# Attention stage of a hybrid decoder step: loads and splits of a group apart, two turned blocks ahead, stores issued by GpSimd, other weights

## The chip, the core and the metric

The kernel runs on one core of a Trainium2 chip. A core has a matrix engine (TensorE, in the profile PE for its matmuls and PEld for its weight loads), three engines for elementwise work (VectorE or DVE, ScalarE or ACT, GpSimd or POOL) and SyncE (SP), which here only issues DMAs. Each engine works through its own queue of instructions strictly in order; an instruction that waits for a semaphore holds up everything behind it on its engine. DMAs can be issued from the queues of SP, ACT and POOL. The metric is the time of one execution on the device in microseconds (us), lower is better.

## What is computed

One inference step of two layers for a prompt of 2048 tokens and, beside it, for 8 decode sequences of 4 new tokens each with 2048 past tokens. Layer 0 has two groups of heads in parallel: HGRN2 (linear attention) and forgetting attention ("fox"); layer 1 is GLA. The change is in the fox attention. Its prompt part and its decode part are:

```python
def fox_prompt(q, k, v, log_f):                    # 4 heads of 128, 2048 tokens
    c = jnp.cumsum(log_f, axis=1).swapaxes(1, 2)
    logits = jnp.einsum('bthd,bshd->bhts', qi, k) * scale + ci[..., None] - c[:, :, None, :]
    logits = jnp.where(t[:, None] >= key_pos[None, :], logits, -jnp.inf)
    p = jax.nn.softmax(logits, axis=-1)
    return jnp.einsum('bhts,bshd->bthd', p, v)

def fox_sample(q, k, v, log_f, k_pages, v_pages, logf_pages, page_table):
    k_past = k_pages[page_table].reshape(db, -1, H, dh)     # 16 pages of 128 rows for each sequence
    v_past = v_pages[page_table].reshape(db, -1, H, dh)
    ...
    p = jax.nn.softmax(jnp.concatenate([logit_past, logit_new], axis=-1), axis=-1)
    return jnp.einsum('bhts,bshd->bthd', p[..., :P], v_past) + jnp.einsum('bhts,bshd->bthd', p[..., P:], v)
```

The outcome is multiplied by a SiLU gate and goes into the output projection of layer 0.

## The kernel before

The program has three phases: the even layer's projections and its HGRN2 heads, then the fox attention (`phase_fox`, L1113), then the output projection of layer 0 and the whole of layer 1. Precision comes from splitting fp32 numbers into two fp16 parts, high and low; a product is then three fp16 matmuls (`mm3`, L450 to L454: high by high, high by low, low by high). Every split is an ACT copy to fp16 and a subtraction of it.

Order. The code writes instructions in program order; a scheduler in the framework then builds the queue of each engine from a simulated timeline, taking among the instructions that are ready the one that stands first in the program. So the order in a queue can differ from the program's. Three tools steer it: `high_priority` puts instructions ahead of all others, `issue_after(x)` keeps what follows behind instruction x in the queue of x's engine (for instructions on that engine alone), and the weights of `mux`, which interleaves two generators: each `yield` gives a cost, and the side whose share of its total (FOX_P for the prompt, FOX_S for the decode part) is behind goes next.

The prompt (`fox_prompt`) runs over 16 groups, 4 heads h by 4 row blocks G of 512 rows. For each group it loads q, k, v (`raw`, 256 KB each, by SP), the bias `cb` and the gate `fsg`, and splits q, k, v (`load_split`, L1131: ACT L1142 and L1143, GpSimd L1144; v is first multiplied on ACT by `self.sv`, a power of two that `y_bounds` works out from the largest |v|, a chain over DVE and PE). `loads` for the next group is called after the first of the group's four blocks of 128 rows. `scores` makes for each block the logits (tile `s`, PE), adds the bias and takes the running maximum on DVE (L1189, with `cm` from GpSimd, L1175), the exponentials on ACT (L1197), and normalises on GpSimd (L1205). `values` turns the probabilities by PE transposes into PSUM (`pt`, L1225, two buffers), splits them (`th` ACT L1232, `tl` DVE L1233) and multiplies them with v (`fo`); it keeps one turned block ahead of the one being multiplied (two, once the decode part has been emitted). The values of a group are interleaved with the scores of the next. The result times the gate (`fy`, DVE L1247) is stored to DRAM (`yT`, L1249) from ACT's queue, the two half-groups at the very end from GpSimd's.

The decode part (`fox_sample`) reads 128 K pages and 128 V pages of 256 KB (SP, L1310; 27 buffers `pg`). Four pages of one sequence make a "quad": 16 PE transposes (`pkt`, L1339), four copies to SBUF (`kts`, ACT L1342 for even heads, DVE L1343 for odd ones), then four sums side by side on the PE array (`sc`, L1397). Once four quads are turned, `past` builds the decay terms; after all 32 quads comes the softmax. Then 34 "strips" (`pv`, L1473) multiply with the V pages, four pages each, as soon as these have landed. `strips` gives the sums `sc` and `pv` high priority.

The mux costs are S0 12000 before the first load, SC_C for each head of a quad, PV_C for each strip; the prompt's costs are about its PE time in ns.

Of the kernel before, what the change touches and what calls it, by code (L numbers as in the profile page):

```python
# [19 lines left out]
P = 128  # L20
# [13 lines left out]
S0 = 12000.0  # L34
SC_C = 700.0
Z_C = 4000.0
# [10 lines left out]
GATE = -9  # L47
PG = 27
PAST = 12
NG = 2  # L50
WSPLIT = 4
FOX_S = 335000.0
FOX_P = 270000.0
# [5 lines left out]
DEC = 4500.0  # L59
PV_C = 4600.0  # L60
NEG = -1e30
# [41 lines left out]
class Kern:  # L103
# [6 lines left out]
    def consts(self):  # L110
        nc, i = self.nc, self.i
        cp = self.ctx.enter_context(self.tc.tile_pool(name="const", bufs=1))
        self.cp = cp

        def col(name, ap, n):
            t = cp.tile([P, n], F32, name=name)
            with nc.allow_non_contiguous_dma(reason="small constant vectors"):
                nc.sync.dma_start(t, ap.rearrange("(k p) -> p k", p=P))
            return t

        self.ident = cp.tile([P, P], F32, name="ident")
# [6 lines left out]
        self.kc, self.n_kc, self.scales = cp.tile([P, 176], F32, name="kc"), 0, {}  # L128
# [108 lines left out]
    def kcol(self, n=1):  # L237
        self.n_kc += n
        assert self.n_kc <= 176
        return self.kc[:, self.n_kc - n : self.n_kc]  # L240
# [209 lines left out]
    def mm3(self, ps, lh, rh, first, last):  # L450
        nc = self.nc
        nc.tensor.matmul(ps, lh[0], rh[0], start=first, stop=False)  # L452
        nc.tensor.matmul(ps, lh[0], rh[1], start=False, stop=False)  # L453
        nc.tensor.matmul(ps, lh[1], rh[0], start=False, stop=last)  # L454

# [318 lines left out]
    def even_half(self, hf, act, wpool, wp, pps, npool, S):  # L774
# [94 lines left out]
        def mk_bkv(hp, which):  # L869
# [74 lines left out]
    def phase_even(self):  # L944
# [4 lines left out]
        with pool("act", side="right") as ap, pool("w", side="right") as w0, pool("wl", side="right") as wp1, \  # L949
# [5 lines left out]
            nrm = Pool(n0, {"th": 1, "nss": 4, "rs_t": 4, "rs_r": 4})  # L955
            self.scales2, self.ready, self.fsc, self.logit = {}, {}, {}, {}
            self.sx_even = self.gain_scale(self.g_even, pps, "pj", "e")
# [155 lines left out]
    def phase_fox(self):  # L1113
        tc, nc = self.tc, self.nc
        with tc.tile_pool(name="fe", bufs=2, reuse_waits="tile") as f1, \
                tc.tile_pool(name="fx", bufs=2, reuse_waits="tile") as f0, \
                tc.tile_pool(name="fpa", bufs=2, space=PSUM, reuse_waits="tile") as pp1, \
                tc.tile_pool(name="fpb", bufs=2, space=PSUM, reuse_waits="tile") as pp0:
            fx = Pool(f0, {"vh": 5, "vl": 5, "P": 17, "th": 3, "tl": 3, "sg": 2, "y": 1},
                      Pool(f1, {"raw": 6, "caus": 1, "qh": 2, "ql": 2, "kh": 5, "kl": 5, "cb": 2, "st1": 12, "cm": 2}))  # L1120
            pps = Pool(pp0, {"t": 2, "o": 1, "kt": 2}, Pool(pp1, {"s": 2, "sc": 1}))
            caus = fx.tile([P, P], F32, tag="caus", name="caus")
            nc.gpsimd.memset(caus, 0.0)
            nc.gpsimd.affine_select(caus, caus, [[-1, P]], ALU.is_ge, FAR, base=0, channel_multiplier=1)
            self.y_bounds(pps)
            with tc.tile_pool(name="fs", bufs=1, side="right", reuse_waits="tile") as s0:
                fs = Pool(s0, {"pg": PG, "kt": 8})
                prompt = self.fox_prompt(fx, pps, caus)
                drain(mux(prompt, FOX_P, self.fox_sample(fs, pps), FOX_S))

    def load_split(self, fx, src, nm, tag, scale=None):  # L1131

        nc = self.nc
        r = fx.tile([P, 512], F32, tag="raw", name=f"raw_{nm}")
        if len(src.shape) == 3:
            nc.sync.dma_start(r.rearrange("p (c d) -> p c d", d=src.shape[2]), src)
        else:
            nc.sync.dma_start(r, src)
        hi = fx.tile([P, 512], F16, tag=tag + "h", name=f"h_{nm}")
        lo = fx.tile([P, 512], F16, tag=tag + "l", name=f"l_{nm}")  # L1140
        if scale is not None:
# [5 lines left out]
    def fox_prompt(self, fx, pps, caus):  # L1147

        nc = self.nc
        cbs, K, V, Q, SG = {}, {}, {}, {}, {}  # L1150
        self.turns = []
        self.sample_done = False

# [7 lines left out]
        def loads(h, G):  # L1161
            gs = slice(G * 512, (G + 1) * 512)
            Q[h, G] = self.load_split(fx, self.qTd[h][:, gs], f"q{h}{G}", "q")
            K[h, G] = self.load_split(fx, self.kTd[h][:, gs], f"k{h}{G}", "k")
            bias(h, G)
            vsrc = self.vd[gs, h * P : (h + 1) * P].rearrange("(c s) d -> s c d", s=P)
            V[h, G] = self.load_split(fx, vsrc, f"v{h}{G}", "v", self.sv[:, 0:1])
            SG[h, G] = fx.tile([P, 512], F32, tag="sg", name=f"fsg{h}{G}")
            nc.sync.dma_start(SG[h, G], self.sgd[h][:, gs])

        def scores(h, G, b):
# [7 lines left out]
            for j in range(G + 1):  # L1179
                w = 512 if j < G else (b + 1) * P  # L1180
                ps = pps.tile([P, 512], F32, tag="s", name=f"s{h}{tb}{j}")
                self.mm3(ps[:, :w], q, [x[:, :w] for x in K[h, j]], True, True)
                lt = fx.tile([P, 512], F32, tag="P", name=f"L{h}{tb}{j}")
# [12 lines left out]
            for j, (lt, w) in enumerate(L):  # L1196
                nc.scalar.activation(lt[:, :w], lt[:, :w], AF.Exp, bias=nm[:, 0:1], scale=ib,  # L1197
                                     accum_out=nm[:, 2 + j : 3 + j])
            if G:
# [8 lines left out]
        def values(h, G, rows, po, b1, b2):  # L1208
# [27 lines left out]
            nj = -(-ns // per)  # L1236
            ahead = [turn(j) for j in range(2 if alone else 1)]
            for j in range(nj):
# [3 lines left out]
                for s, a, c0 in parts:  # L1242
                    vv = [x[:, (s % 4) * P : (s % 4 + 1) * P] for x in V[h, s // 4]]
                    self.mm3(po[:, c0:c2], vv, [x[:, a : a + c2 - c0] for x in (th, tl)], s == 0, s == ns - 1)
                yield sum(c2 - c0 for _, _, c0 in parts) * 2.1
            y = fx.tile([P, 512], F32, tag="y", name=f"fy{h}{G}{b1}")
            nc.vector.scalar_tensor_tensor(y[:, c1:c2], po[:, c1:c2], self.sv[:, 2:3], SG[h, G][:, c1:c2], ALU.mult,  # L1247
                                           ALU.mult)
            (nc.scalar if c2 - c1 == 512 else nc.gpsimd).dma_start(self.yT[0][NH + h][:, G * 512 + c1 : G * 512 + c2], y[:, c1:c2])  # L1249

        groups = [(h, G) for h in range(NH) for G in range(4)]
        loads(0, 0)
        pv, ns = iter(()), 0
# [29 lines left out]
    def fox_sample(self, fs, pps):  # L1283
# [118 lines left out]
        for n in range(4 * DB + 1):  # L1402
            if n < 4 * DB:
# [91 lines left out]
    def fox_scale(self, which, hp):  # L1495


        nc = self.nc
        c = self.scales[f"B{which}{hp}"][:, 2:3]
        up, down = self.fsc[which, hp] = self.kcol(), self.kcol()  # L1500
        nc.vector.tensor_scalar(down, c, 2.0**19, 2.0**-20, ALU.mult, ALU.max)
        if which == "q":
            nc.vector.tensor_scalar(up, c, 2.0**20, 2.0**-19, ALU.mult, ALU.min)
            nc.vector.tensor_scalar(up, up, SCALE, None, ALU.mult)
            return
        nc.vector.reciprocal(up, down)

        ib, beta = self.logit[hp] = self.kcol(), self.kcol()
# [3 lines left out]
    def y_bounds(self, pps):  # L1512
# [17 lines left out]
        most(f, ("Bg0", "Bg1"))  # L1530
        vm, self.sv = self.spread(self.vmax[:, :NPG], pps, "kt", "vm"), self.kcol(3)
        nc.vector.tensor_scalar(f, f, vm, 0.5, ALU.mult, ALU.mult)

        self.power2(vm, 2.0**14, self.sv)
        nc.vector.tensor_scalar(self.sv[:, 2:3], self.sv[:, 1:2], 2.0**-15, None, ALU.mult)
        nc.vector.tensor_tensor(f, f, b, ALU.max)
# [370 lines left out]
```

## Time and profile before

| | us |
|---|---|
| median of 3 runs | 2438.14 (2437.21 to 2438.71) |
| the profiled execution | 2438.64 |
| its span, first to last instruction | 2436.6 |
| mean granted TensorE clock | 0.987 |

The fox stage lies between about 880 and 1332 us of the span. In the rows below, a view by windows gives for each stretch its length and then for each engine the busy time and the number of instructions, then the granted clock, the mean busy share of the DMA engines and GB/s. A view of waits has engine, line and tile that waited, what it waited for, the total in us, how often, and the longest. A timeline row has start, length, engine, line, operation and, in brackets, the idle time of the engine before it and what ended it.

### The profile page before, as it was taken

The numbers are of one execution on the slowest core, as the hardware profiler recorded it, in microseconds if no ns is written. First come the engines' busy times: TensorE is split into PE (matmuls) and PEld (weight loads), VectorE is DVE, ScalarE is ACT, GpSimd is POOL, SyncE is SP. The second block draws the span as 40 slices with busy tenths as digits, with TensorE's granted clock in tenths as the row PEclk, the third lists the DMA queues.
The fourth block names the chain that finished last, engine by engine and source line by source line (L and its number), as shares of the span: only waits on it lengthen the run. The fifth ranks groups of instructions, "written<-read, shape, count | busy, mean of one in ns | idle before, by whom it ended". The sixth has DMA issues, their size and how long they took to land. (4 is left out here: it accounts for less than half of the span.)

```text
span 2436.6 us, 54263 instructions
## 1 busy us (share of the span) xinstructions
PE 2314.2 (95%) x21116; PEld 1642.6 (67%) x21116; DVE 1459.8 (60%) x3337; ACT 1141.4 (47%) x2513; POOL 750.2 (31%) x825
## 2 busy tenths in 40 slices
PE   7999999999999989999788999999999999998998
PEld 5667668855655876666345776777778766666887
DVE  7666656446765637777557353665675555557564
ACT  6434343343433137766457454445553645545243
POOL 2223223012213225443334220432443222322233
PEclk9999999999999999999999999999999999999999
DMA  6222235435431277666684631222146312114454
GB/s 178 78 80 70 76 104 171 144 106 141 148 114 59 85 230 257 207 191 212 224 261 143 198 107 44 62 75 75 63 143 186 125 36 67 47 58 152 141 195 152
DMA packets 297955, 316.96 MB, mean 130 GB/s; under 512 B 39729, under 2 KB 241010, under 8 KB 297698
## 3 DMA queue, kind: packets, MB, share of 16 engines
q1 hardware_dynamic: 295234, 308.98, 40.5%
q8 instruction: 166, 2.72, 0.5%
q10 hardware_dynamic: 2160, 3.93, 0.4%
q14 instruction: 91, 0.75, 0.1%
q0 software_dynamic: 304, 0.59, 0.1%
HBM read 242.31 MB, written 71.11 MB: 129 GB/s over the span
## 5 line engine op out<-in xcount | busy, mean ns | idle before, releaser
L452 PE MATMUL pt_o<-w_o,act 128*128 128x256 f16 x1024 | 282.9, 277 | 2.4 <-ACT w_o L334 1.4
L453 PE MATMUL pt_o<-w_o,act 128*128 128x256 f16 x1024 | 283.2, 277 | 0.9 <-POOL w_o L335 0.9
L454 PE MATMUL pt_o<-w_o,act 128*128 128x256 f16 x1024 | 283.2, 277 | 0.0
L452 PEld LDWEIGHTS <-act 128*128 128x128 f16 (+1 forms) x2320 | 229.0, 99 | 41.7 <-issue 10.7
L453 PEld LDWEIGHTS <-act 128*128 128x128 f16 (+1 forms) x2320 | 228.8, 99 | 33.5 <-issue 2.9
L454 PEld LDWEIGHTS <-act 128*128 128x128 f16 (+1 forms) x2320 | 228.8, 99 | 33.0 <-issue 4.4
L454 PE MATMUL pt_Cv<-w_Cv,act 128*128 128x256 f16 (+1 forms) x520 | 142.4, 275 | 0.0
L452 PE MATMUL pt_Cv<-w_Cv,act 128*128 128x256 f16 (+1 forms) x520 | 142.2, 275 | 0.0
L453 PE MATMUL pt_Cv<-w_Cv,act 128*128 128x256 f16 (+1 forms) x520 | 142.0, 275 | 0.0
L631 POOL TENSOR_TENSOR kA<-kA,fA 128x512 f32<-128x512 f32 (+1 forms) x56 | 80.4, 1436 | 197.3 <-PE gl_A L597 112.5
L631 POOL TENSOR_TENSOR kC<-kC,fC 128x512 f32<-128x512 f32 (+1 forms) x56 | 84.5, 1509 | 157.2 <-PE gl_C L597 76.6
L1197 ACT ACTIVATE L<-L,nm,kc 128x512 f32<-128x512 f32 (+3 forms) x160 | 118.2, 741 | 30.5 <-DVE nm L1195 26.0
L1205 POOL TENSOR_SCALAR L<-L,nm 128x512 f32<-128x512 f32 (+3 forms) x160 | 97.9, 628 | 95.4 <-DVE nm L1201 34.2
L1232 ACT ACTIVATE th<-pt 128x512 f16<-128x512 f32 (+3 forms) x159 | 82.0, 527 | 86.8 <-PE pt L1225 76.7
L1233 DVE TENSOR_TENSOR tl<-pt,th 128x512 f16<-128x512 f32 (+3 forms) x159 | 95.2, 608 | 42.4 <-ACT th L1232 40.9
L1339 PEld LDWEIGHTS pkt<-ident,pgcache_fox_k 128*128 128x128 f32 x512 | 60.1, 144 | 45.6 <-issue 24.8
L1339 PE MATMUL pkt<-ident,pgcache_fox_k 128*128 128x128 f32 x512 | 78.4, 282 | 10.8 <-DMA pgcache_fox_k<-in_cache_fox_k 5.3
L1225 PE MATMUL pt<-ident,L 128*128 128x128 f32 x544 | 88.1, 276 | 0.0
L1225 PEld LDWEIGHTS pt<-ident,L 128*128 128x128 f32 x544 | 68.0, 143 | 22.3 <-issue 1.2
L452 PE MATMUL pt_Bv<-w_Bv,act 128*128 128x256 f16 (+2 forms) x264 | 72.2, 273 | 0.0
L454 PE MATMUL pt_Bv<-w_Bv,act 128*128 128x256 f16 (+2 forms) x264 | 72.2, 273 | 0.0
L453 PE MATMUL pt_Bv<-w_Bv,act 128*128 128x256 f16 (+2 forms) x264 | 72.2, 273 | 0.0
(1088 smaller groups left out, 6863.3 us busy)
## 6 DMA issues: line engine op xcount, KB each, us to landing
pgcache_fox_k<-in_cache_fox_k SPq DMA_DIRECT2D x128, 256.0 KB, 4.1
pgcache_fox_v<-in_cache_fox_v SPq DMA_DIRECT2D x128, 256.0 KB, 3.6
yr<-yT SPq DMA_DIRECT2D x16, 1024.0 KB, 5.8
nx<-in_x_prompt SPq DMA_DIRECT2D x16, 512.0 KB, 5.1
wr_Aqf<-in_w_in_even SPq DMA_DIRECT2D x64, 128.0 KB, 2.8
wr_o<-in_w_out_even SPq DMA_DIRECT2D x32, 256.0 KB, 4.0
wr_Cv<-in_w_in_odd SPq DMA_DIRECT2D x32, 256.0 KB, 4.2
wr_Cqk<-in_w_in_odd SPq DMA_DIRECT2D x64, 128.0 KB, 2.6
```

The lines of the kernel that those rows point to most:

```text
L452: nc.tensor.matmul(ps, lh[0], rh[0], start=first, stop=False)
L453: nc.tensor.matmul(ps, lh[0], rh[1], start=False, stop=False)
L454: nc.tensor.matmul(ps, lh[1], rh[0], start=False, stop=last)
L631: nc.gpsimd.tensor_tensor(kv[:, :, 0], kv[:, :, 0], t1.to_broadcast([P, nb, w]), ALU.mult)
L1197: nc.scalar.activation(lt[:, :w], lt[:, :w], AF.Exp, bias=nm[:, 0:1], scale=ib, accum_out=nm[:, 2 + j : 3 + j])
L1205: nc.gpsimd.tensor_scalar(lt[:, :w], lt[:, :w], nm[:, 1:2], 2.0**14, ALU.mult, ALU.mult)
L1225: nc.tensor.transpose(pt[:, w : w + P], rows[b][s // 4][0][:, (s % 4) * P : (s % 4 + 1) * P], self.ident)
L1232: nc.scalar.activation(th[:, a:w], pt[:, a:w], AF.Copy),
L1233: nc.vector.tensor_tensor(tl[:, a:w], pt[:, a:w], th[:, a:w], ALU.subtract)))
L1339: nc.tensor.transpose(pk[:, j * P : (j + 1) * P], pgs[j][:, h * P : (h + 1) * P], self.ident)
```

## The change

Loads and splits of a prompt group become two functions. The loads stay after the first block of the group before; the splits of q and k are emitted after its third block, that of v after its fourth. Each is placed behind the last exponentials emitted so far (`last_exp`) and behind the last K copy of head 2 emitted so far by the decode part (`last_kt`); both are ACT instructions, so the rule binds ACT's queue. v is scaled by a factor known from the weights (`fox_scale("v", ..)`, worked out in the even phase) instead of one from the measured maximum, and `y_bounds` moves from the start of the stage into the decode part, behind `past`. `values` keeps two turned blocks ahead from the start, with `th` and `tl` in 4 buffers instead of 3. All stores of `fy` are issued by GpSimd. The gate tile `fsg` gets 3 buffers instead of 2, and the pages 25 instead of 27. SC_C goes from 700 to 800, PV_C from 4600 to 5860, FOX_S from 335000 to 411000. `last_pe` is recorded in `scores` and `values`; nothing in the program reads it, and `strips` is as it was.

```diff
-SC_C = 700.0
+SC_C = 800.0
-PG = 27
+PG = 25
-FOX_S = 335000.0
+FOX_S = 411000.0
-PV_C = 4600.0
+PV_C = 5860.0
...
-                if which == "k" and hf == 0:
-                    self.fox_scale("k", hp)
+                if hf == 0:
+                    self.fox_scale(which, hp)
...
-            fx = Pool(f0, {"vh": 5, "vl": 5, "P": 17, "th": 3, "tl": 3, "sg": 2, "y": 1},
+            fx = Pool(f0, {"vh": 5, "vl": 5, "P": 17, "th": 4, "tl": 4, "sg": 3, "y": 1},
...
-            self.y_bounds(pps)
...
-    def load_split(self, fx, src, nm, tag, scale=None):
...
+    def load(self, fx, src, nm):
+        r = fx.tile([P, 512], F32, tag="raw", name=f"raw_{nm}")
+        self.nc.sync.dma_start(r.rearrange("p (c d) -> p c d", d=src.shape[2]) if len(src.shape) == 3 else r, src)
+        return r
+
+    def split(self, fx, r, nm, scale=None):
...
-            Q[h, G] = self.load_split(fx, self.qTd[h][:, gs], f"q{h}{G}", "q")
-            K[h, G] = self.load_split(fx, self.kTd[h][:, gs], f"k{h}{G}", "k")
+            raw["q"] = self.load(fx, self.qTd[h][:, gs], f"q{h}{G}")
+            raw["k"] = self.load(fx, self.kTd[h][:, gs], f"k{h}{G}")
             bias(h, G)
-            vsrc = self.vd[gs, h * P : (h + 1) * P].rearrange("(c s) d -> s c d", s=P)
-            V[h, G] = self.load_split(fx, vsrc, f"v{h}{G}", "v", self.sv[:, 0:1])
+            raw["v"] = self.load(fx, self.vd[gs, h * P : (h + 1) * P].rearrange("(c s) d -> s c d", s=P), f"v{h}{G}")
...
+        def split(which, h, G):
+
+            with ExitStack() as st:
+                for x in (self.last_exp, self.last_kt):
+                    if x is not None:
+                        st.enter_context(self.tc.issue_after(x.ins))
+                r = self.split(fx, raw[which], f"{which}{h}{G}", self.fsc["v", h // 2][0] if which == "v" else None)
+                {"q": Q, "k": K, "v": V}[which][h, G] = r
...
-            ahead = [turn(j) for j in range(2 if alone else 1)]
+            ahead = [turn(j) for j in range(min(2, nj))]
...
-            (nc.scalar if c2 - c1 == 512 else nc.gpsimd).dma_start(self.yT[0][NH + h][:, G * 512 + c1 : G * 512 + c2], y[:, c1:c2])
+            nc.gpsimd.dma_start(self.yT[0][NH + h][:, G * 512 + c1 : G * 512 + c2], y[:, c1:c2])
...
                 rows.append((yield from scores(h, G, b)))
-                if b == 0 and j + 1 < len(groups):
-                    loads(*groups[j + 1])
+                if j + 1 < len(groups):
+                    if b == 0:
+                        loads(*groups[j + 1])
+                    elif b == 2:
+                        split("q", *groups[j + 1])
+                        split("k", *groups[j + 1])
+                    elif b == 3:
+                        split("v", *groups[j + 1])
...
                     new.append(turn(c, b, h, pgs))
+                    if h == 2:
+                        self.last_kt = new[-1][1]
                     yield SC_C
...
             if n == PAST // NH:
                 yield from past()
+                self.y_bounds(pps)
```

More of the change, by code (lines that the diff above doesn't have):

```diff
@@ L126, in consts @@
         self.g_even = col("g_even", i["norm_even"][0], KT)
-        self.kc, self.n_kc, self.scales = cp.tile([P, 176], F32, name="kc"), 0, {}
+        self.kc, self.n_kc, self.scales = cp.tile([P, 184], F32, name="kc"), 0, {}
         self.vmax = cp.tile([P, NPG], F32, name="vmax")
@@ L453, in mm3 @@
         nc.tensor.matmul(ps, lh[0], rh[1], start=False, stop=False)
-        nc.tensor.matmul(ps, lh[1], rh[0], start=False, stop=last)
+        return nc.tensor.matmul(ps, lh[1], rh[0], start=False, stop=last)
     def proj_fm(self, pps, act, W, off, M, hf, evac, nm):
@@ L1129, in phase_fox @@
                 drain(mux(prompt, FOX_P, self.fox_sample(fs, pps), FOX_S))
-    def load_split(self, fx, src, nm, tag, scale=None):
-        nc = self.nc
[L1134 to L1140, printed above, removed]
+    def load(self, fx, src, nm):
[3 more added lines that the diff above has]
+    def split(self, fx, r, nm, scale=None):
+        nc = self.nc
+        hi = fx.tile([P, 512], F16, tag=nm[0] + "h", name=f"h_{nm}")
+        lo = fx.tile([P, 512], F16, tag=nm[0] + "l", name=f"l_{nm}")
         if scale is not None:
@@ L1149, in fox_prompt @@
         nc = self.nc
-        cbs, K, V, Q, SG = {}, {}, {}, {}, {}
+        cbs, K, V, Q, SG, raw = {}, {}, {}, {}, {}, {}
         self.turns = []
-        self.sample_done = False
+        self.sample_done, self.last_exp, self.last_kt = False, None, None
         def bias(h, g):
@@ L1181, in scores @@
                 ps = pps.tile([P, 512], F32, tag="s", name=f"s{h}{tb}{j}")
-                self.mm3(ps[:, :w], q, [x[:, :w] for x in K[h, j]], True, True)
+                self.last_pe = self.mm3(ps[:, :w], q, [x[:, :w] for x in K[h, j]], True, True)
                 lt = fx.tile([P, 512], F32, tag="P", name=f"L{h}{tb}{j}")
@@ L1506, in fox_scale @@
         nc.vector.reciprocal(up, down)
+        if which == "v":
+            self.v_undo[hp] = self.kcol()
+            nc.vector.tensor_scalar(self.v_undo[hp], down, 2.0**-15, None, ALU.mult)
+            return
         ib, beta = self.logit[hp] = self.kcol(), self.kcol()
@@ L1530, in y_bounds @@
         most(f, ("Bg0", "Bg1"))
[L1531 to L1535, printed above, removed]
+        nc.vector.tensor_scalar(f, f, self.spread(self.vmax[:, :NPG], pps, "kt", "vm"), 0.5, ALU.mult, ALU.mult)
         nc.vector.tensor_tensor(f, f, b, ALU.max)
```

15 lines of the change are left out of this document (9 added, 6 removed).

## Prediction

> **What bounds the kernel now.** I read the page first, then busy time by stage, then the waits, then the queues of the engines that the change touches.
>
> ```profile
> span 2436.6 us, 54263 instructions
> PE 2314.2 (95%) x21116; PEld 1642.6 (67%) x21116; DVE 1459.8 (60%) x3337; ACT 1141.4 (47%) x2513; POOL 750.2 (31%) x825
> ...
> 1330.85 0.52 ACT act L1569
> ```
>
> The last row is the first piece of the chain of waits. The chain runs from 1330.9 us to the end, 1105.7 us, and all of it lies behind the fox stage, in code that the change leaves alone. So I take the time after the stage as fixed and ask when the stage ends. By stretches (length, then PE, PEld, DVE, ACT, POOL busy, clock, DMA share, GB/s):
>
> ```profile
> 880.00:905.00 25.00, 15.18 (x123) 12.27 (x121) 10.59 (x55) 9.63 (x19) 11.24 (x13) 0.85 0.98 319
> 905.00:1085.00 180.00, 174.75 (x1249) 113.07 (x1247) 133.90 (x399) 126.66 (x287) 86.62 (x144) 0.98 0.69 223
> 1085.00:1152.00 67.00, 63.65 (x490) 40.83 (x492) 47.74 (x146) 46.16 (x105) 33.17 (x50) 1.00 0.71 225
> 1152.00:1166.00 14.00, 13.28 (x117) 8.28 (x106) 11.31 (x40) 9.46 (x20) 2.92 (x5) 1.00 0.21 74
> 1166.00:1283.00 117.00, 96.22 (x642) 42.50 (x641) 62.59 (x207) 53.98 (x125) 42.66 (x67) 0.99 0.79 252
> 1283.00:1332.00 49.00, 40.77 (x281) 29.30 (x281) 35.72 (x98) 33.95 (x73) 17.93 (x28) 0.97 0.38 115
> ```
>
> PE is idle 9.8 us in the head, 5.3 and 3.4 while K pages are turned, 20.8 while V pages are summed and 8.2 in the tail, some 48 us with the softmax stretch. Nothing that only removes waits can give more than about that. DVE and ACT are busy 74% and 70% in the K stretch, so three engines share the load there.
>
> ```profile
> PE pv L1473 <- DMA pgcache_fox_v<-in_cache_fox_v: 17.4, 13, 2.3
> PE fo L452 <- ACT th L1232: 4.7, 5, 3.3
> PE fo L453 <- DVE tl L1233: 3.8, 11, 0.5
> ...
> L1310 SPq DMA_DIRECT2D pgcache_fox_k<-in_cache_fox_k x128: 327/333/1234, 899.7 to 1103.2; - x128
> ...
> L1310 SPq DMA_DIRECT2D pgcache_fox_v<-in_cache_fox_v x128: 332/333/893, 1103.8 to 1277.2; - x128
> ...
> 1180.58 27.19 SPq L1310 DMA_DIRECT2D pgcache_fox_v<-in_cache_fox_v  x27
> ...
> SPq L1310 <- PE pkt L1339: 66.2, 46, 5.6
> ```
>
> The first three are PE's waits from 905 to 1332. In the V stretch PE waits for pages, and the pages wait for SP: 27 issues in 27.19 us without a pause, 1.01 us a page, 4.03 us for the four of a strip. With 27 buffers full at 1166, the other 101 pages need 102 us; the stretch lasts 117. In the K stretch it is the other way round: SP waits 66.2 us until PE has turned a page. So the supply of V sets one stretch, and the mixture on PE, DVE and ACT the other.
>
> **The change part by part.** The profiled execution took 2438.64 us, 2.0 more than its span and 0.5 more than the median of the runs shown.
>
> *Head of the stage.* The timelines of ACT and DVE:
>
> ```profile
> 888.00 0.63 ACT L1143 ACTIVATE h_k<-raw_k 128x512 f16<-128x512 f32 x1
> 892.14 0.63 ACT L1143 ACTIVATE h_k<-raw_k 128x512 f16<-128x512 f32 x1 [3.50 <-DMA raw_k<-kTd]
> 894.60 1.95 ACT L1142 ACTIVATE raw_v<-raw_v,kc 128x512 f32<-128x512 f32 x3 [1.83 <-DVE kc L1535]
> 899.60 0.63 ACT L1143 ACTIVATE h_k<-raw_k 128x512 f16<-128x512 f32 x1 [3.06 <-DMA raw_k<-kTd]
> 900.14 1.65 ACT L1143 ACTIVATE h_v<-raw_v 128x512 f16<-128x512 f32 x3
> 901.70 0.48 ACT L1197 ACTIVATE L<-L,nm,kc 128x128 f32<-128x128 f32 x1
> ...
> 891.81 0.69 DVE L897 TENSOR_REDUCE vmax<-Bv 128x1 f32<-128x512 f32 x1
> ...
> 894.41 0.15 DVE L257 RECIPROCAL kc<-kc 128x1 f32<-128x1 f32 x1
> ...
> 896.53 0.28 DVE L1189 CUSTOM_DVE_ANT_0 L<-s,cm 128x128 f32<-128x128 f32 x1
> ```
>
> ACT splits k and v of later groups, waits for their loads in between, and comes to the first exponential at 901.7. DVE is through with the projections at 892.5 and then does the chain of `y_bounds` until 896.5, while the first logits wait in PSUM. After the change later splits stand behind the exponentials, and the chain stands behind `past`; the first exponential can come near 893.2 (892.5, the 0.28 us of L1189 and its small followers). That is 8.5 us. But the first page is only issued at 899.7, and PE needs it for more than small early groups. Bounds 0 and -8.5; I take -6, because the chain and the splits ahead both go. `y_bounds` itself costs DVE the same 4 us later, hidden beside a DVE at 74%, and 4 without that cover. The new factor for v adds some three DVE instructions of 0.15 us for each pair of heads to the projections: under 1 us, behind their matmuls.
>
> *Splits that wait for loads, later on.* ACT's waits from 905 to 1332:
>
> ```profile
> ACT raw_v L1142 <- DMA raw_v<-vd: 12.2, 8, 2.7
> ACT th L1232 <- DMA yT<-fy: 4.8, 1, 4.8
> ACT h_k L1143 <- DMA raw_k<-kTd: 3.1, 3, 2.0
> ACT h_q L1143 <- DMA raw_q<-qTd: 2.7, 1, 2.7
> ```
>
> Two or three blocks after the issue the loads have landed, so 18.0 us (12.2 + 3.1 + 2.7) of ACT waiting go. PE idles only 8.6 us in the two K stretches, so between 0 and -8.6 reach the end; I take -3, as ACT is not the last engine there.
>
> *Two turned blocks ahead.* `fo` waits 8.5 us for `th` and `tl`; another turn in between covers most of it. Bounds 0 and -8.5, I take -4.
>
> *Stores by GpSimd.*
>
> ```profile
> L1249 ACTq DMA_DIRECT2D yT<-fy x15: 326/347/362, 922.0 to 1310.6; - x15
> L1249 POOL DMA_DIRECT2D yT<-fy x2: 562/573/584, 1323.5 to 1332.9; - x2
> ...
>   DVE fy L1247: 7.3, 1
> ```
>
> ACT loses 15 issues of 0.347 us, 5.2 in all, and the wait of 4.8 above. GpSimd gets 15 of 0.573, 8.6 us in a stage where it is under half busy. The wait for `fy` moves too: behind it on GpSimd stand `cm` (DVE's next logits), L1205 (the next transposes) and the low halves of the splits. The one such wait on GpSimd was 7.3 us, in the tail. Bounds +7.3 and -5; I take -1, since before it stood on the busier engine.
> The Trainium skill speaks against this move: "SBUF — State Buffer", section "Who interferes with whom", says that a GpSimd-issued DMA has its descriptors written through ports that some DVE instructions lock, and the page's example is 620 ns alone against about 3100 beside a DVE copy. Worked out as an estimate, 15 stores 2.5 us later would be 37 us of GpSimd, and with a tenth of it on the path the sum would be 4 us higher. The two stores above took 0.573 us, which shows no such wait, but they are only two; the sum goes by the row.
>
> *Buffers.* Two pages fewer are in store when the V strips begin, and these come at 1.01 us: +2. A split that comes later holds its `raw` tile longer, but six of them serve two groups and a load is only called one group ahead, so nothing on SP's queue waits for it. The third `fsg` buffer spares SP waits for `fy`, which lie in the K stretch where SP waits for PE anyway: nothing.
>
> *Weights and the order behind `last_kt`.* This is the largest step. Adding the yields, the K turns are all emitted at 12 + 128 times 0.8 + about 6 of the decode part's 411 thousand, when the prompt stands at 79 of its 233; the split for the first group of head 2 comes at 94. So all K copies of even heads go ahead of it on ACT. Before they did not:
>
> ```profile
> 1087.10 0.22 PE L452 MATMUL s<-h_k,h_q 128*128 128x128 f16 x1
> ...
> L1342 ACT ACTIVATE kts<-pkt x64: 572/595/619, 907.2 to 1148.9; 128x512 f32<-128x512 f32 x64
> ...
> 880.00:1085.00 205.00, 57.13 (x368) 43.84 (x368) 30.91 (x45) 27.07 (x46) 0.97 0.73 235
> 1085.00:1152.00 67.00, 21.31 (x144) 16.26 (x144) 13.05 (x19) 10.60 (x18) 1.00 0.71 225
> ...
> 1085.00:1152.00 67.00, 19.59 (x73) 2.25 (x3) 1.00 0.71 225
> ...
> 1283.00:1332.00 49.00, 25.22 (x135) 1.98 (x3) 0.97 0.38 115
> ```
>
> The first row is the first logit of head 2 (240 `s` matmuls belong to the heads before it). The last copy on ACT came 62 us later. The windows of `pkt` say that 368 of 512 turns were done by 1085: 9 quads were left, and the last 67 us of K also held 73 `fo` matmuls (the fifth row). After the change the prompt waits for K: the K stretch ends earlier, near 1100, the V stretch moves forward with it, and prompt work moves into the tail. If scheduler and engines mix as well as before, nothing is lost. If the prompt stands still while K finishes, 9 quads need 36 us at SP's pace, and the 73 matmuls need 40 us at the tail's rate (135 in 49 us, 90 of them half as wide, so 90 whole ones), 76 in place of 67: +9; the same stop at the groups before, where quads 11, 18, 24 and 29 are due, may double that. Below nothing: prompt work without page waits beside it could gain as much as it loses, -9. Bounds -9 and +18; I take +4, as the row of 1085 to 1152 with PE 95% busy is hard to beat.
>
> Sum: -6 -3 -4 -1 +2 +4 = -8, from 2438.64 to 2430.6; against the median of the runs, 2430.
>
> **The rivals.** *K alone (slower).* The order behind `last_kt` leaves PE to a K chain that SP feeds at 4.03 us a quad: +18, with the pages' +2, and of the gains of -14 some -11 stays, as PE then waits for K and not for ACT: +9, 2447. For it: the 62 us between the two rows above, and a rule on ACT alone that ties the prompt to the decode part. Against it: K has first claim on the engines anyway, and a throttled prompt still fills most of PE. It decides once the idle PE time up to the last K copy is over some 25 us (19 before: 9.8, 5.3, 3.4).
> *Strips spread out (faster).* A strip now costs 5860 of 411000, that is 3.85 us of prompt against 3.71, and would meet its pages: most of the 17.4 us of page waits go, 2430 less 16 is 2414. Against it: the strips stand by high priority and by when the simulated pages land, not by the mux, and `last_pe` is read by nothing. The decode sums are then no more and no less behind the prompt than before.
> *Nothing moves.* Waits taken from ACT come back as waits for DVE, at 74%, and V's supply still lasts 102 us: 2438.
>
> **How the numbers follow.** Forecast 2430 with its own range of 2424 to 2438 (the smaller terms half way to their bounds, not all at once): 0.45. K alone, 2447: 0.28. Strips spread, 2414: 0.13. Nothing moves, 2438: 0.14. A measurement of this kernel can tell about 0.2%, 5 us, from no change. Faster by more than that: 0.38 of the forecast, 0.13 of the spread, 0.01 of nothing, together 0.52. Within: 0.06 of the forecast and 0.11 of nothing, 0.17. Slower: 0.28 of K alone, 0.01 of the forecast and 0.02 of nothing, 0.31. The range reaches from 2407 (the forecast with the low ends of the turned blocks, ACT's waits and the order) to 2454 (K alone, with the longest wait of a store on top).
>
> **What would show it.** The first exponential near 893 and a clock above 0.85 in the first 25 us; no ACT wait on `raw` beyond a few us; the last `kts` near 1100 instead of 1148.9, ahead of the first logits of head 2; the V stretch still some 105 to 117 us with about 17 us of page waits, but ending near 1235; a tail of about 90 us in place of 49. It would be wrong if the last `kts` stays near 1149, if the V stretch shortens by more than its 102 us of supply allow, if GpSimd's stores take over 1 us, or if the tail runs so much below the K stretch that the gains of the head are gone.

## The result and the profile after

| | before | after |
|---|---|---|
| median of 4 runs each, us | 2438.43 | 2452.26 (2449.41 to 2455.06) |
| ratio, 95% interval | 1 | 1.0055 (1.004 to 1.007) |
| profiled execution / its span | 2438.64 / 2436.6 | 2449.7 / 2448.0 |

The change made the kernel 13 to 14 us slower; the forecast was 8 faster. The stretches of the stage by the view of windows of the changed kernel (length, PE, PEld, DVE, ACT, POOL busy, clock, DMA share, GB/s), cut where K ends, where the V strips begin and where they end:

```profile
880.00:905.00 25.00, 16.16 (x115) 12.48 (x113) 7.59 (x29) 7.78 (x17) 10.39 (x16) 0.80 1.00 324
905.00:1111.00 206.00, 192.59 (x1421) 120.39 (x1420) 139.13 (x403) 122.60 (x273) 78.22 (x130) 0.99 0.70 230
1111.00:1129.00 18.00, 16.80 (x138) 10.01 (x137) 14.66 (x47) 12.10 (x27) 7.47 (x12) 1.00 0.35 104
1129.00:1254.00 125.00, 102.64 (x678) 45.07 (x676) 68.63 (x233) 66.54 (x154) 57.66 (x87) 0.98 0.84 272
1254.00:1345.00 91.00, 80.76 (x521) 52.53 (x514) 72.14 (x226) 68.76 (x156) 48.13 (x73) 0.97 0.26 83
```

From 905 to the first strip it now takes 224 us (261 before), the V stretch 125 (117), the tail 91 (49): -37, +8, +42. The K stretch really became shorter; what it lost in length is prompt work, and that came back in the tail with interest. PE idles 13.4 us in the K stretch, 22.4 in the V stretch and 10.2 in the tail. In the tail PE is busy 89%, DVE 79% and ACT 76%: only prompt work is left there, and each of its blocks goes through PE, DVE, ACT and GpSimd in turn. Which of them sets its pace wasn't tested.

Where K runs alone, first PE and then ACT by their timelines (start, length, operation, in brackets the idle time before it and what ended it):

```profile
1038.39 1.09 PE L1356 MATMUL pkt<-ident,pgcache_fox_k 128*128 128x128 f32 x8
1039.83 1.09 PE L1356 MATMUL pkt<-ident,pgcache_fox_k 128*128 128x128 f32 x8 [0.35 <-DVE kts L1360]
1041.27 1.06 PE L1414 MATMUL sc<-kts,qz 128*32 128x512 f32 x8 [0.35 <-DVE kts L1360]
1042.26 1.09 PE L1356 MATMUL pkt<-ident,pgcache_fox_k 128*128 128x128 f32 x8
1043.70 1.09 PE L1356 MATMUL pkt<-ident,pgcache_fox_k 128*128 128x128 f32 x8 [0.35 <-DVE kts L1360]
1044.63 0.38 PE L452 MATMUL s<-h_k,h_q 128*128 128x512 f16 x1
...
1041.02 0.60 ACT L1359 ACTIVATE kts<-pkt 128x512 f32<-128x512 f32 x1 [0.84 <-PE pkt L1356]
1043.45 0.60 ACT L1359 ACTIVATE kts<-pkt 128x512 f32<-128x512 f32 x1 [1.84 <-PE pkt L1356]
1043.94 0.62 ACT L1143 ACTIVATE h_q<-raw_q 128x512 f16<-128x512 f32 x1
1044.46 0.62 ACT L1143 ACTIVATE h_k<-raw_k 128x512 f16<-128x512 f32 x1
```

Turn, turn, sum: a quad every 3.9 to 4.0 us, and ACT waits for PE between two copies. The split of the next group's q stands right behind a K copy, and the group's first logit starts 0.7 us after it. How much prompt work PE had in this stretch, by windows of the tiles `s` (first row) and `fo` (second row) of the changed kernel:

```profile
1028.00:1047.00 19.00, 0.72 (x3) 0.00 (x0) 1.00 0.87 287
1028.00:1047.00 19.00, 0.00 (x0) 0.00 (x0) 1.00 0.87 287
```

Three `s` matmuls, no `fo`, beside 72 turns of K; a1, below, has 21 and 24 in the same 19 us, beside 36 turns. The head, the K copies on ACT, the stores, and the waits of PE and GpSimd from 905 to 1345:

```profile
890.68 0.49 ACT L1205 ACTIVATE L<-L,nm,kc 128x128 f32<-128x128 f32 x1 [5.44 <-DVE nm L1203]
897.73 0.69 PE L1356 MATMUL pkt<-ident,pgcache_fox_k 128*128 128x128 f32 x2 [6.68 <-DMA pgcache_fox_k<-in_cache_fox_k]
L1359 ACT ACTIVATE kts<-pkt x64: 571/597/606, 901.8 to 1111.8; 128x512 f32<-128x512 f32 x64
L1258 POOL DMA_DIRECT2D yT<-fy x17: 557/584/794, 913.9 to 1346.1; - x17
PE pv L1493 <- DMA pgcache_fox_v<-in_cache_fox_v: 18.2, 12, 2.6
PE fo L452 <- ACT th L1240: 5.8, 6, 1.9
PE fo L453 <- DVE tl L1241: 1.7, 5, 0.5
POOL yT L1258 <- DVE fy L1256: 18.4, 8, 5.4
```

The first exponential comes 11 us sooner, 2.7 of them because the stage itself began sooner in this execution (first split of q at 879.0, before at 881.7). But PE stands still for 6.7 us, up to 897.7, for the first K page. The last K copy on ACT is 37 us sooner. A store costs GpSimd 0.584 us.

### The profile page after: what moved, and what is told of

Its sections match the earlier page's. It is cut to its first block, busy times and chain, and to the rows that moved or that the text cites. A ratio compares the mean times of both kernels' runs of the same rounds, so it can differ in the third digit from the quotient of the medians.

```text
span 2448.0 us, 54349 instructions
## 1 busy us (share of the span) xinstructions
PE 2316.9 (95%) x21116; PEld 1637.8 (67%) x21116; DVE 1463.7 (60%) x3339; ACT 1140.1 (47%) x2513; POOL 759.4 (31%) x840
## 4 chain that ended last, share of the span: by engine, by line
PE 71%; DVE 9%; DMA 8%; ACT 5%; issue 3%; POOL 2%; SPq 2%; POOLq 0%; DVEq 0%; ACTq 0%
PE pt_o L452 3%; PE pt_o L454 3%; PE pt_o L453 3%; PE pkt L1356 2%; PE pt_Cv L452 2%; PE pt_Cv L453 2%; PE pt_Cv L454 2%; DMA pgcache_fox_v<-in_cache_fox_v 2%; PE pt L1233 2%; PE sc L1414 1%; ACT L L1205 1%; PE pf_Ag L452 1%; PE pf_Ag L454 1%; PE pf_Bq L453 1%; PE pf_Ag L453 1%
```

## The experiments

Eighteen runs. "Ratio" is to the kernel before on the same chip, with its 95% interval. Runs of one kernel spread by 5 to 22 us, so terms of 2 or 3 us can't be told one by one. The theory to begin with: the edge behind the K copies makes the prompt stand still and costs the time there. Its rivals: the new weights, the stores or the two blocks, and that nothing holds the decode sums behind the prompt.

| run | edit (from the changed kernel unless said) | median us | ratio |
|---|---|---|---|
| a1 | no edge behind the K copies | 2432.28 | 0.9979 (0.9966 to 0.9993) |
| a2 | decode sums behind the prompt | 2435.54 | 0.9988 (0.9975 to 1.0001) |
| a3 | old weights | 2466.03 | 1.0117 (1.0094 to 1.0139) |
| a6 | one block ahead | 2451.97 | 1.0060 (1.0041 to 1.0080) |
| a2b | a1 and a2 together | 2438.50 | 0.9999 (0.9985 to 1.0014) |
| m2 | a2 with matched weights | 2437.14 | 0.9995 (0.9977 to 1.0013) |
| a7 | a1, `y_bounds` first | 2439.65 | 0.9997 (0.9982 to 1.0012) |
| a5 | a1, stores by ACT | 2437.72 | 0.9991 (0.9979 to 1.0003) |
| e4 | kernel before with the edge alone | 2445.07 | 1.0032 (1.0016 to 1.0048) |
| m3 | matched weights | 2449.48 | 1.0050 (1.0033 to 1.0067) |
| a3n | a1 with old weights | 2441.07 | 1.0013 (1.0000 to 1.0026) |
| h1 | a1, S0 30000 | 2434.18 | 0.9983 (0.9972 to 0.9993) |
| s3 | early splits, old weights | 2451.11 | 1.0049 (1.0033 to 1.0065) |
| s1 | early splits | 2443.94 | 1.0018 (1.0007 to 1.0029) |
| m4 | a1 with matched weights | 2437.41 | 0.9998 (0.9983 to 1.0013) |
| s2 | s1 and a2 together | 2434.01 | 0.9977 (0.9968 to 0.9987) |
| h2 | a1, first K quad behind the prompt | 2429.31 | 0.9957 (0.9940 to 0.9973) |
| a1_again | a1 on another chip | 2435.23 | 0.9992 (0.9980 to 1.0004) |

### Which part costs it: a1, a2, a3, a6

```diff
a1
-                for x in (self.last_exp, self.last_kt):
+                for x in (self.last_exp,):
a2
-        with self.tc.high_priority():
+        with ExitStack() as st:
+            st.enter_context(self.tc.issue_after(self.last_pe.ins))
+            st.enter_context(self.tc.high_priority())
a3
-SC_C = 800.0
+SC_C = 700.0
-FOX_S = 411000.0
+FOX_S = 335000.0
-PV_C = 5860.0
+PV_C = 4600.0
a6
-            ahead = [turn(j) for j in range(min(2, nj))]
+            ahead = [turn(j) for j in range(2 if alone else 1)]
```

> The changed kernel with the splits of a group placed behind the last exponentials alone, no longer behind the last K copy of head 2. Theory E (the order behind the K copies stops the prompt while K quads run alone, about 29 us of prompt time at 1019 to 1048 and twice 6 to 8 us later): the standstill at 1019 to 1048 goes, the last K copy comes near 1149 again, the tail behind the last strip is some 50 to 60 us, time 2430 to 2438. Theory W (the new weights and 25 pages cost it): no change, 2449 to 2455. Theory S (stores by GpSimd or two blocks ahead cost it): no change, 2449 to 2455. Theory Q (the sums of the decode part are not held behind the prompt, whatever the splits do): at most 5 us off, 2446 to 2452.

> The changed kernel with the sums of the decode part (sc and pv) placed behind the last prompt matmul emitted so far (last_pe, which the changed kernel records and does not use); the order of the splits stays. Theory Q: K can no longer run ahead alone, strips meet their pages, page waits of PE fall from 18 to under 8 us, the prompt does not stand still, time 2425 to 2438. Theory E: the splits still wait for K copies, and K is held as well, so the standstill stays or grows: 2449 to 2465. Theories W and S: 2449 to 2455.

> The changed kernel with SC_C 700, PV_C 4600 and FOX_S 335000 as before; 25 pages and all else of the change stay. Theory W: back to 2435 to 2441. Theory E: by the old weights the K turns are all emitted at about 108 of 335 thousand, when the prompt stands at 75 of 233 instead of 79, hence the same standstill before the first group of head 2, 2446 to 2456. Theories S and Q: 2447 to 2455.

> The changed kernel with one turned block ahead until the decode part has been emitted, as before (four buffers of th and tl stay). Prediction's step (two ahead is worth 4 us, at most 8.5): 2453 to 2461, with waits of fo for th and tl up from 7.5 to some 8 to 14 us. Theory S (two ahead crowd ACT and DVE ahead of the K copies): 2440 to 2448. Theories E and W: no change beyond 5 us, 2448 to 2457.

Without the edge the loss is gone: 2432.3 in place of 2452.3. The windows of a1, cut in the same way:

```profile
905.00:1154.00 249.00, 241.84 (x1747) 153.74 (x1744) 189.15 (x583) 175.09 (x403) 124.93 (x200) 0.99 0.64 209
1154.00:1167.00 13.00, 13.00 (x119) 8.49 (x118) 10.51 (x31) 8.61 (x17) 3.41 (x6) 1.00 0.37 119
1167.00:1287.00 120.00, 97.08 (x624) 41.09 (x622) 62.41 (x205) 54.02 (x126) 47.50 (x72) 0.94 0.79 255
1287.00:1323.00 36.00, 32.02 (x244) 24.05 (x237) 28.27 (x81) 25.23 (x55) 12.54 (x20) 1.00 0.40 131
```

K and softmax take 262 us again, the tail 36 (50 to 60 were expected). PE idles 7.2, 22.9 and 4.0 us. But a2 keeps the edge and gets the loss back as well. Its windows:

```profile
905.00:1126.00 221.00, 207.40 (x1550) 129.08 (x1547) 152.82 (x447) 135.83 (x301) 84.61 (x140) 0.98 0.66 218
1126.00:1293.00 167.00, 156.49 (x985) 77.16 (x983) 113.11 (x387) 110.66 (x259) 92.32 (x141) 0.96 0.68 223
1293.00:1326.00 33.00, 28.07 (x208) 21.50 (x205) 24.98 (x69) 21.15 (x45) 12.00 (x19) 0.95 0.37 117
```

Its first stretch is that of the changed kernel: 221 us with 13.6 us of idle PE, 224 with 14.6. So the K copies still hold the prompt up: from 1028 to 1047 PE has 9 `s` matmuls and no `fo`. The difference lies behind: the strips are spread over 167 us and the tail is 33, together 200 us, with 15.4 us of idle PE; in the changed kernel 216 with 32.6. No wait of `pv` for a page is left among PE's waits there. So the put-off prompt work can be made good behind K: in the changed kernel it found no room beside strips that run as soon as pages land, and lay over into the tail. That doesn't make the standstill free. Against a1 the changed kernel has 7 us more idle PE up to the first strip and 6 more in the tail. a2 keeps the first and saves 17 behind it, about as much as its lost page waits (18.2 us in the changed kernel), which a1 and the kernel before pay as well (21.3 and 17.4).

The old weights are worse by 14 us, not better, which refutes the new weights as the cause; 2466 lies above every range expected. One block ahead changes nothing (its waits of `fo` are 11.4 us for `th` and `tl`, 7.5 with two).

### One loss or two: a2b, m2; the small terms: a7, a5

```diff
a2b: the edits of a1 and of a2
m2: the edit of a2, and
-SC_C = 800.0
+SC_C = 1500.0
-PV_C = 5860.0
+PV_C = 3300.0
a7: the edit of a1, and
-                self.y_bounds(pps)
...
+            self.y_bounds(pps)
             with tc.tile_pool(name="fs", bufs=1, side="right", reuse_waits="tile") as s0:
a5: the edit of a1, and
-            nc.gpsimd.dma_start(self.yT[0][NH + h][:, G * 512 + c1 : G * 512 + c2], y[:, c1:c2])
+            (nc.scalar if c2 - c1 == 512 else nc.gpsimd).dma_start(self.yT[0][NH + h][:, G * 512 + c1 : G * 512 + c2], y[:, c1:c2])
```

> The changed kernel without the edge behind the K copies (as a1) and with the decode sums behind the prompt (as a2). Theory 1, two separate losses (the standstill beside K costs some 18 us, strips that run ahead of their pages cost 16 by PE's idle time in the V stretch): both gains add up, 2412 to 2420, page waits of pv under 5 us, the last strip near 1290 to 1300. Theory 2, one loss with two cures (prompt work is put off by the edge and is paid only because the strips leave it no room; either cure alone makes it good): 2428 to 2436.

> The changed kernel with the edge kept, the decode sums behind the prompt, and weights that put the K turns where they run without the edge: SC_C 1500 (all K turns emitted at 210 of 411 thousand, the prompt at 138 thousand, where the run without the edge ends K at 133 to 143) and PV_C 3300 (a strip each 2.2 thousand of prompt, the last at 216 of 233). If the edge costs only because the weights put K turns ahead of the pace that PE, ACT and DVE hold: no standstill, the last K copy near 1150, page waits under 5 us, 2412 to 2424. If waiting behind a K copy costs by itself, whatever the weights: 2430 to 2445.

> The kernel without the edge (a1, 2432.3) with the chain of y_bounds put back at the start of the stage. The prediction's head step (4 of its 6 us are this chain): first exponential 4 us later, 2435 to 2438. Theory P (PE waits 6.6 us for the first K page, so an early first exponential only lengthens that wait): the wait for the first page falls to 2 to 4 us and the time stays, 2431 to 2434.

> The kernel without the edge (a1, 2432.3) with the fifteen whole stores issued by ACT again. The prediction's step (-1 for GpSimd): 2432 to 2435, and 15 waits or issues back on ACT. The Trainium skill, "SBUF — State Buffer", section "Who interferes with whom", would have it the other way (stores by GpSimd cost some 4 us): 2428 to 2430. The trace of the changed kernel, with 0.584 us a store, speaks for the first.

The two cures don't add up: a2b is no faster than either, and slower than both theories had it. PE's waits from 905 to 1335 in a2b, and the windows of its V stretch:

```profile
PE pv L1495 <- DMA pgcache_fox_v<-in_cache_fox_v: 20.7, 18, 2.1
...
1178.00:1300.00 122.00, 96.80 (x626) 40.51 (x625) 61.50 (x203) 55.13 (x124) 47.34 (x72) 0.97 0.82 268
```

The page waits stay at 20.7 us, so here the edit holds the strips back from nothing. A likely reason, not tested by itself: without the edge the prompt runs ahead (360 of its 480 `s` matmuls are done when the first strip starts, 240 in a2), and a prompt matmul that a sum was placed behind has long run. Then edge and held sums belong together: the edge keeps K and prompt at their places in the program, and only then does holding the strips space them. It also means that a2b doesn't decide between one loss and two, as it has no held strips. m2 has edge and held sums with other weights and is no faster than a2: its page waits fall to 6.8 us, but PE idles 16.2 us from 905 to the first strip. In a7 the first exponential is at 897.7 and PE's waits for the first pages fall from 7.3 to 3.2 us. By their medians a7 and a5 lie above all that was expected, but a1 ran on other chips, and by the ratios they differ from a1 and a1_again by less than the intervals. Neither term is decided.

### Why the edge is dear: e4, m3, a3n, m4, s3, s1, s2

```diff
e4 (from the kernel before)
+        with ExitStack() as st:
+            if self.last_kt is not None:
+                st.enter_context(self.tc.issue_after(self.last_kt.ins))
...
+                    if h == 2:
+                        self.last_kt = new[-1][1]
m3: SC_C 1500, PV_C 3300; m4: the same and the edit of a1
a3n: the edits of a3 and of a1
s1 (s3: with the edit of a3, s2: with that of a2)
-                    elif b == 2:
-                        split("q", *groups[j + 1])
-                        split("k", *groups[j + 1])
-                    elif b == 3:
-                        split("v", *groups[j + 1])
+                    elif b == 1:
+                        for x in "qkv":
+                            split(x, *groups[j + 1])
```

> The kernel before with one part of the change alone: the ACT part of every split is placed behind the last K copy of head 2 emitted so far. All else as before (loads and splits together, one block ahead, stores by ACT, old weights, 27 pages). Theory E (the edge is the cause): quads of K follow one another at about 4 us with no prompt work between, the last K copy comes near 1110 to 1126 in place of 1149, the tail is some 90 us, 2450 to 2466 (the changed kernel with these weights took 2466.0). Rival (the edge costs only together with another part, the late splits or two blocks ahead): 2436 to 2443.

> The changed kernel with SC_C 1500 and PV_C 3300 alone, the edge kept and the decode sums not held behind the prompt. If the edge costs because the weights place the K turns ahead of their pace: no standstill, last K copy near 1150 to 1165, tail 25 to 50 us, 2432 to 2440. If the edge costs by itself: 2445 to 2455.

> The changed kernel with the old weights and without the edge. With the edge the old weights were 14 us slower than the new (2466.0 against 2452). If weights act only through the edge: 2430 to 2440. If the old weights are worse by themselves for late splits and two blocks ahead: 2444 to 2450.

> The changed kernel with the old weights and the edge (2466.0 as it was), its splits emitted after the second block of the group before and not after its third and fourth. Theory L (a late split leaves one block of slack behind a K copy, so the edge stops the prompt; the edge alone in the kernel before, with three blocks of slack, cost 7): 2442 to 2452. Rival (the edge costs the same wherever the split stands; the rest of the 21 us between that run and this kernel lies elsewhere): 2460 to 2468.

> The changed kernel, edge kept, its splits emitted after the second block of the group before. Theory L: the standstill of the prompt shrinks to under 15 us in one piece, 2436 to 2445. Rival (slack does not matter): 2448 to 2455.

> The changed kernel with SC_C 1500 and PV_C 3300 and without the edge; the same weights with the edge took 2449.5. If it is the edge itself that costs there: 2432 to 2439. If it is these weights: 2445 to 2452.

> The changed kernel, edge kept, with the early splits of s1 and the decode sums behind the prompt (2435.5 with late splits). If the standstill beside K and the tail are separate losses: some 10 us below the run with late splits, 2423 to 2429. If holding the sums already makes good what the standstill put off: 2432 to 2438.

The edge by itself, by the ratios, as these runs were on different chips: 15 to 19 us with the new weights (changed kernel against a1_again and a1), 25 with the old (a3 against a3n), 13 with weights that place the K turns where they run anyway (m3 against m4), 8 in the kernel before (e4, between the two ranges expected). So it costs whatever the weights; m3 was a miss of the theory that weights alone make it bind. e4 shows the picture of the changed kernel with no other part of the change: last K copy at 1115.8, first strip at 1129.7, last `fo` matmul at 1344.5 (1331.8 before).

The price seems to go by how late the split stands: with the splits emitted after the second block and not after the third and fourth, the kernel is 8 us faster with the new weights (s1) and 15 with the old (s3). No run has early splits without the edge, so a gain of early splits by themselves isn't excluded; that a1, with late splits, is no slower than the kernel before, with early ones, speaks against it. The windows of s1:

```profile
905.00:1119.00 214.00, 205.83 (x1554) 130.63 (x1553) 150.99 (x446) 137.19 (x302) 88.14 (x144) 1.00 0.71 232
1119.00:1244.00 125.00, 103.39 (x685) 45.86 (x683) 68.01 (x233) 63.20 (x150) 52.79 (x82) 0.97 0.84 272
1244.00:1338.00 94.00, 81.10 (x519) 52.74 (x516) 74.21 (x227) 69.33 (x158) 49.97 (x77) 0.98 0.25 76
```

The K stretch gains 10 us against the changed kernel, 6.4 of it idle PE, at the same number of PE instructions; V stretch and tail stay (125 and 94, with 125 and 91 in the changed kernel). Holding the sums on top (s2) shortens those, but 2434.0 can't be told from a2's 2435.5: the 10 us beside K didn't add to it, as the second case of the expectation had it. By the traces the time from the first exponential to the first strip is 6 us shorter in s2 than in a2 and the strips take 4 longer; why is open. That the old weights are 14 us worse is in part their own (a3n against a1 and a1_again: 5 to 8 us by the ratios); the rest acts through the edge and wasn't followed up.

### The head: h1, h2, a1_again

```diff
h1: the edit of a1, S0 30000, FOX_S 429000
h2: the edit of a1, and
-S0 = 12000.0
+S0 = 4000.0
...
                 for h in range(NH):
-                    new.append(turn(c, b, h, pgs))
+                    with ExitStack() as st:
+                        if n == 0:
+                            st.enter_context(self.tc.issue_after(self.last_pe.ins))
+                        new.append(turn(c, b, h, pgs))
```

> The kernel without the edge (a1, 2432.3) with S0 30000 in place of 12000 (and FOX_S 429000, so that all later steps keep their places within some thousandths): the first K turn is placed behind some 18 thousand of prompt work in place of 8. Theory P (the head's gain is lost as PE waits 6.6 to 7.3 us for the first K page): that wait goes, 2425 to 2430. Rival (the wait is paid elsewhere, as K starts and ends later by as much): 2431 to 2437.

> The kernel without the edge (a1) with the turns of the first K quad placed on PE behind the prompt matmuls emitted so far (and S0 4000, so that these are few); with S0 30000 the scheduler had still put the first turn ahead and PE waited 6.6 us. Theory P (the head's gain is lost because PE stands at the first K page): the wait of PE for that page falls below 1.5 us and the time is 4 to 6 us below that of a1 on the same chip. Rival (K, started later, ends later by as much, or other waits of the first small groups take the place): within 2.5 us of a1.

> The kernel without the edge once more, on the chip of the run beside it: 2430 to 2438, ratio 0.997 to 0.9995. It tells whether the changed kernel without the edge is faster than the kernel before (0.9979 on the first chip) or whether the small terms of the prediction came to nothing (1.0000).

h1 doesn't decide: the scheduler still put the first turn ahead, and PE waited 6.6 us. In h2 the order on PE is what was meant, by its timeline:

```profile
902.95 0.63 PE L453 MATMUL fo<-tl,h_v 128*128 128x512 f16 x1
903.38 0.63 PE L454 MATMUL fo<-th,l_v 128*128 128x512 f16 x1
903.80 1.91 PE L1356 MATMUL pkt<-ident,pgcache_fox_k 128*128 128x128 f32 x8
```

PE no longer waits for a K page up to 945 us, and h2 is 5.9 us below a1 on the same chip: 2429.31, ratio 0.9957. That is faster than the kernel before and the changed one. The gain lies where it was expected: by windows PE idles 9.4 us from 880 to the end of K, 16.7 in a1_again. S0 was changed with it, so the two are not told apart.

## Why the prediction was wrong, point by point

*The order behind `last_kt` is the step that failed.* The sum gave it +4, with bounds of -9 and +18; taking it out gives 15 to 19 us by the ratios (1.0055 against 0.9992 in a1_again and 0.9979 in a1). Much of its picture was right: the last K copy came at 1112 (1100 foreseen), the tail was 91 us (90 foreseen), with 18.2 us of page waits before it (17 foreseen). But the V stretch took 125 us (105 to 117) and the strips ended at 1254 (1235). The working for a prompt that stands still (36 us of K, 40 of tail, in place of 67, and the same again at the groups before) came out at +18, near the measured size, in part by luck: it let the last 9 quads run alone, but from 1092 to 1112 PE did 16 `s` and 18 `fo` matmuls beside them. The long stop was earlier, at 1028 to 1047, at the second group of head 1, and 8 us of the loss came in the V stretch. What failed was the choice of +4 between the ends, by "If scheduler and engines mix as well as before, nothing is lost" and a gain of 9 that was held as likely as a loss. The put-off work could not be made good in the V stretch, since its strips go as soon as pages land: it held 642 PE instructions in 117 us before, 678 in 125 after, and 985 in 167 once the sums were held (a2).

*The rival K alone* had sign and nearly the size (2447, measured 2452), but not the place. It was to decide at over 25 us of idle PE up to the last K copy; head and K stretch had 8.8 and 13.4, some 22. Of the 13 us by which PE idles more in the changed kernel than in a1, 7 lie up to the first strip and 6 in the tail; a tail that eats up the head's gains was the last of the prediction's signs of being wrong.

*Strips spread out* needed a queue behind the prompt, as the prediction said; with it a2 gains 17 us, about the 16 that the rival counted, but from 2452 and not from 2430.

*The head*, -6: the first exponential came at 890.7, as foreseen (893.2) once the 2.7 us are taken off by which the stage began sooner, but the clock in the first 25 us was 0.80, not above 0.85, and PE then stood 6.7 us for the first page. The prediction named that page and left it in the bound; it was the next thing late. By h2 about 6 us were there.

*The time after the stage* was taken as fixed, and for the changed kernel that held: from its last `fo` matmul to the end of the span are 1103.6 us, 1104.8 before. It need not hold where the stage ends sooner. The last `fo` matmuls of the kernel before and PE's wait behind them, by the views of the tile and of the waits:

```profile
L454 PE MATMUL fo<-th,l_v x174: 219/379/634, 914.1 to 1331.8; 128*128 128x512 f16 x99, 128*128 128x256 f16 x43, 128*128 128x128 f16 x17, 128*128 128x384 f16 x15
...
PE pt_o L452 <- ACT w_o L334: 1.4, 1, 1.4
```

and of a1:

```profile
L454 PE MATMUL fo<-th,l_v x174: 217/379/635, 904.5 to 1322.3; 128*128 128x512 f16 x99, 128*128 128x256 f16 x43, 128*128 128x128 f16 x17, 128*128 128x384 f16 x15
...
PE pt_o L452 <- ACT w_o L334: 5.1, 1, 5.1
```

The stage of a1 ends 9.5 us sooner (1331.8, 1322.3), its span is 5.7 shorter (2436.6, 2430.9): 3.7 of the rest is the longer wait for the weights of the output projection, which ACT splits. In the ten traces where that wait is 4.5 to 5.1 us (a1, a1_again, a2, a2b, m2, m3, a7, a5, s2, h2) the time behind the last `fo` is 1107.8 us in the mean (1103.0 to 1115.0), in the other ten, with 1.4 to 1.9 us of it, 1103.8 (1100.7 to 1106.7). So part of a gain in the stage seems to be given back, but single executions scatter by more than the wait.

*The other small terms.* ACT's waits for raw loads are gone from 905 on, two blocks ahead came to nothing in the changed kernel (a6; -4 foreseen), and GpSimd's stores took 0.584 us each with waits for `fy` of 18.4 us in all, the longest 5.4 (under the bound of 7.3). The lockout of which the Trainium skill warns ("SBUF — State Buffer", section "Who interferes with whom") isn't seen in that row. Head, waits, blocks, stores and buffers together were to give -12, so they were too large as well; a1 gives -5 (0.9979) on one chip and -2 (0.9992) on another.

*Still open:* of the 22 us between the stage in the changed kernel (465 us) and in a1 (443), 13 are idle time of PE, named above, and 3 an earlier start of the stage in that execution; the rest is in PE's busy time and wasn't placed.

## What to carry to other kernels

An order that ties one stream to another can cost twice, at the wait and where the work that it puts off ends. So price the last stretch too, where that work runs alone. Two orders can be halves of one idea: the edge alone cost 15 to 19 us, the order behind the prompt held no strip back without it, and with both the kernel was level with one that has neither. Where an instruction is freed to come earlier, look up what stands next in the queue of the engine that it feeds: here it was a turn that waited for a page, and moving that turn (with S0) was worth 6 us, against 2 to 5 for all the rest of the change without the edge.

## What the runs showed of the hardware

The granted clock is no constant of a stretch: in the V stretch it is 0.99 in the kernel before, 0.98 in the changed one, 0.96 in a2 and 0.94 in a1. What sets it wasn't tested, nor what it costs: the V stretch of a1 is 3 us longer than that before, at 97.1 and 96.2 us of busy PE. The mean clock moves with the spread between runs of one kernel: of the seven runs of h2 the fastest took 2421.06 us at a mean clock of 0.989, the slowest 2435.13 at 0.985.
